# A transformer trunk on one core: four weight sums of the down projection move from VectorE to POOL, and the last three k tiles of the last product are taken result by result

## The chip, the cores and the metric

The kernel runs on one core of one Trainium2 chip. The metric is the device time of one execution in microseconds. The engines named below are TensorE (PE, matrix products), VectorE (DVE), ScalarE (ACT), GpSimd (POOL) and SyncE (SP, which issues the DMAs here).

## The reference

One layer of a hybrid decoder trunk on x of 2048 tokens by 1024 features, in f32: a mixer (matrix memory, attention and spatial gating side by side), and then a feed-forward network with a causal convolution, both gated and added to x. What matters here is the end of it:

```python
D_FF = 11 * D_MODEL // 4                      # 2816
def conv_ffn(h, w_up, w_conv, b_conv, w_down):
    z = h @ w_up
    z = causal_depthwise_conv(z, w_conv, b_conv)
    a, gv = jnp.split(z, 2, axis=-1)
    return (jax.nn.silu(a) * gv) @ w_down
...
        h = rms_norm(x, g_ffn[l]) * (1.0 + sc2) + sh2
        x = x + gt2 * conv_ffn(h, w_up[l], w_conv[l], b_conv[l], w_down[l])
```

The down projection is the last matrix product, (2048 x 2816) by (2816 x 1024).

## The kernel before

The tokens are taken in two halves H of 1024. For each half, class `Down` computes the product of the activations (1024 x 2816) and the weight (2816 x 1024) as a 2 x 2 block product with seven block products in place of eight (Strassen's scheme in Winograd's form). A block of activations is named (i, j): i is the block of 512 tokens, j the half of the 2816 rows of the sum. A quarter of the weight is (i, j) with i the half of those rows and j the block of 512 output columns. The products run in the order 1, 2, 7, 6, 5, 4, 3, and each runs over KH = 11 k tiles of 128 rows. One step is one (H, product p, k tile).

To keep f32 accuracy, each operand tile (128 x 512) is split into a high half (rounded, by ACT, `A.copy`, L1489) and a low half (the rest, by DVE, L1490), and `mm3` (L54 to L56) makes three matmuls: high by high, high by low, low by high. A step has four results i (128 tokens each, one PSUM bank each) of three matmuls: 12 matmuls a step, 132 a product.

Four methods share a step's work:

- `load` issues the DMAs of the weight tiles, tag `wd`, eight buffers; product 7 needs two tiles to a step, the others one.
- `prep` makes the two operands and their halves. Products 1 and 2 take them as they were loaded. Product 7 takes the difference of two activation blocks (L1468, into `sw`) and of two weight quarters (L1470, into `t2w`, one tile for each k tile, kept). Product 6 changes activations in place (L1473, L1474) and adds a weight quarter to `t2w` (L1475). Products 5 and 4 subtract `t2w` from the loaded weight tile in place (L1478, L1481). Product 3 changes activations in place (L1484). All these run on DVE. The halves lie in tag `wsp`, twelve buffers, four to a step.
- `mm` makes the matmuls. Product 3 goes on summing in the banks of product 5.
- `post` queues what is done with a finished product's results: product 1's are copied by ACT (L1543); those of 2, 5 and 4 take three DVE instructions each (L1524 with one operand from PSUM, L1528, L1529) and a store; those of 7 one (L1549, from PSUM); those of 6 four (L1554 and L1555, from PSUM, L1579, L1580); those of 3 two (L1568, from PSUM, L1569) and a store to `out`.

The main loop (L1659 on) walks the steps: loads six steps ahead, `prep` three steps ahead (AHEAD = 3), then the matmuls, then up to three queued pieces of the results. A scheduler orders each engine's instructions by this order and by its own estimates of time, and allots the buffers of each tag. After the last step the four results of product 3 are finished (`last`, L1565 to L1570).

Of the kernel before, what the change touches and what calls it, by code (L numbers as in the profile page):

```python
# [12 lines left out]
ALU = mybir.AluOpType  # L13
# [20 lines left out]
def trunk(  # L34
# [7 lines left out]
    V, A, G, T = nc.vector, nc.scalar, nc.gpsimd, nc.tensor  # L42
# [10 lines left out]
    def mm3(ps, lh, ll, rh, rl, start, stop, resume=False):  # L53
        T.matmul(ps, lh, rh, start=start, stop=False, skip_group_check=resume)  # L54
        T.matmul(ps, lh, rl, start=False, stop=False, skip_group_check=resume)  # L55
        T.matmul(ps, ll, rh, start=False, stop=stop, skip_group_check=resume)  # L56
# [266 lines left out]
    def half2(tag):  # L323
        return (
            pool.tile([P, 512], F32R, name=tag + "h", tag=tag),
            pool.tile([P, 512], F32R, name=tag + "l", tag=tag),
        )
# [273 lines left out]
    def products(i, mm):  # L601

        w = nxt[0]
        for k in range(KT):
            mm(k)
            if k == 3 and wide[0]:
                tick(True)
            if w and i == 7:
                if k in (0, 1, 2, 5):
                    w.cast()  # L610
                if k == 0:
                    w.load()
        if w and i <= 3:
            w.load()
        if w and 4 <= i <= 6:
            w.cast()
            w.load()
        tick()
# [16 lines left out]
    def natural(half, wb, consume):  # L635
        wide[0] = wb.width == 512
        for i in range(8):
            tt = half * 8 + i
            tb, o = tt // 4, (tt % 4) * P
            ps = acc_ps()  # L640

            def mm(k):
                hh, hl = hT[tb, k]
                mm3(ps[:, : wb.width], hh[:, o : o + P], hl[:, o : o + P], *wb.tiles[k], k == 0, k == KT - 1)

            products(i, mm)
            consume(tt, ps)
# [544 lines left out]
    class Block:  # L1192
# [10 lines left out]
        def mm(self, i, nb):  # L1203
            if i not in self.x:
                self.x[i] = pool.tile([P, D], F32, name="x2")
                dma(self.x[i], x[self.rows(i), :])
                self.st[i] = pool.tile([P, 2], F32, name="st", tag="wst_")
            sl = slice(i * P, (i + 1) * P)
            ps = self.ps[i, nb] = pp.tile([P, 512], F32, name="wps")
            for k in range(KT):  # L1210
                mm3(ps, self.y[k][0][:, sl], self.y[k][1][:, sl], *wo[nb * 8 + k], k == 0, k == KT - 1)
# [116 lines left out]
    class Group:  # L1328
# [12 lines left out]
        def prep(self, p):  # L1341
            A_ = self.A
            n = OF[p]
            if (self.H, self.g) == (0, 0) and (0, n) not in hb:
                b_first(n)
            if p in (5, 6) and self.S1 is None:
                self.S1, self.S2 = self.tmp("S1", "sw"), self.tmp("S2", "sw")
                V.tensor_tensor(self.S1, A_[2, 1], A_[2, 2], op=ALU.add)
                V.tensor_tensor(self.S2, self.S1, A_[1, 1], op=ALU.subtract)
            if p == 7:  # L1350
                V.tensor_tensor(self.S1, A_[1, 1], A_[2, 1], op=ALU.subtract)
            elif p == 3:
                V.tensor_tensor(self.S2, A_[1, 2], self.S2, op=ALU.subtract)
            src = {1: A_[1, 1], 2: A_[1, 2], 4: A_[2, 2]}.get(p)
            if src is None:
                src = self.S1 if p in (5, 7) else self.S2
            hi, lo = half2("wsp")
            A.copy(hi, src)  # L1358
            V.tensor_tensor(lo, src, hi.bitcast(F32), op=ALU.subtract)  # L1359
            self.wa[p] = hi, lo  # L1360
# [67 lines left out]
    KH = 11  # L1428
    n_bank = [0]

    class Down:
# [29 lines left out]
        def prep(self, p, k):  # L1461
            a = lambda i, j: self.act(i, j, k)
            B = self.B.pop((p, k))
            if p in (1, 2):
                av, bv = a(1, p), B[0]
            elif p == 7:
                av = self.tmp("sw")
                V.tensor_tensor(av, a(1, 1), a(2, 1), op=ALU.subtract)  # L1468
                bv = self.T2[k] = self.tmp("t2w")
                V.tensor_tensor(bv, B[0], B[1], op=ALU.subtract)  # L1470
            elif p == 6:

                V.tensor_tensor(a(2, 1), a(2, 1), a(2, 2), op=ALU.add)  # L1473
                V.tensor_tensor(a(1, 1), a(2, 1), a(1, 1), op=ALU.subtract)  # L1474
                V.tensor_tensor(self.T2[k], self.T2[k], B[0], op=ALU.add)  # L1475
                av, bv = a(1, 1), self.T2[k]
            elif p == 5:
                V.tensor_tensor(B[0], B[0], self.T2[k], op=ALU.subtract)  # L1478
                av, bv = a(2, 1), B[0]
            elif p == 4:  # L1480
                V.tensor_tensor(B[0], B[0], self.T2[k], op=ALU.subtract)  # L1481
                av, bv = a(2, 2), B[0]
            else:
                V.tensor_tensor(a(1, 2), a(1, 2), a(1, 1), op=ALU.subtract)  # L1484
                av, bv = a(1, 2), B[0]
            halves = []
            for v in (av, bv):
                hi, lo = half2("wsp")
                A.copy(hi, v)  # L1489
                V.tensor_tensor(lo, v, hi.bitcast(F32), op=ALU.subtract)  # L1490
                halves += [hi, lo]
            self.sl[p, k] = halves

        def mm(self, p, k):
            more = p == 3
            if k == 0:
                if more:
                    self.ps[3] = self.ps[5]
                else:
                    n_bank[0] += 1  # L1500
                    tag = "db%d" % ((n_bank[0] - 1) % 2)
                    self.ps[p] = [pp.tile([P, 512], F32, name="db", tag=tag) for _ in range(4)]
            ah, al, bh, bl = self.sl.pop((p, k))
            for i in range(4):
                sl = slice(i * P, (i + 1) * P)
                mm3(self.ps[p][i], ah[:, sl], al[:, sl], bh, bl, not more and k == 0, k == KH - 1, resume=more)

        def rest(self, ti, nl, i):

# [134 lines left out]
    for i in range(AHEAD):  # L1644
        up_groups(-1)
    prep(0)
    blk.evict(2, 1)
    blk.stats(2)
    prep(1)
    blk.scale(2, True)  # L1650
    blk.evict(3, 1)
# [3 lines left out]
    blk.scale(3, True)  # L1655
    b_first("B21", (3,))
    prep(2)
    loaded = n_open + 1
    for i, s in enumerate(steps):  # L1659
# [86 lines left out]
```

## Time and profile before

| | |
|---|---|
| median of 3 runs | 2607.7 us (2606.87 to 2610.26) |
| profiled execution, time | 2607.8 us |
| profiled execution, span | 2606.1 us |
| granted TensorE clock, mean | 0.997 |
| PE busy | 2530.5 us (97%) |
| DVE busy | 2010.0 us (77%) |
| ACT busy | 1272.8 us (49%) |
| POOL busy | 402.5 us (15%) |

The span runs from the first instruction to the end of the last; the time of the profiled execution is 1.7 us longer and is the one to set beside the median. Busy times overlap between engines. Matmuls are pipelined and their ends are modelled, so that each shows 0.39 us although the next one begins 0.23 us after it. A line L54 to L56 is that of the helper `mm3`, so groups are told apart by their tiles: `db` is the down projection's result, `wsph` and `wspl` its high and low halves, `act` its activations, `wd` and `t2w` its weight tiles.

### The profile page before, as it was taken

The page shows a single profiled execution, that of the slowest core. Times are in us where ns is not written, and L with a number is a line of the kernel's source. Part 1 is how long each engine was busy: PE and PEld are TensorE (multiplying, and loading weights), DVE is VectorE, ACT ScalarE, POOL GpSimd, SP SyncE. Part 2 cuts the span into 40 slices and gives each one's busy share as a digit, 9 for nine tenths or more (in the row PEclk, how much of TensorE's full clock was granted, in tenths as well). Part 3 has the DMA queues.
Part 4 walks back from the last instruction along what each step waited for, and adds up shares of the span by engine and source line. Part 5 has one row for each costly group of instructions (what it writes and reads, how often), then busy time and mean ns, then how long its engine had stood idle before and what let it go on. Part 6 is the DMA issues. An engine that isn't in the chain of part 4 may idle for free.

```text
span 2606.1 us, 36311 instructions
## 1 busy us (share of the span) xinstructions
PE 2530.5 (97%) x12521; PEld 2097.9 (81%) x12537; DVE 2010.0 (77%) x3438; ACT 1272.8 (49%) x2424; POOL 402.5 (15%) x532
## 2 busy tenths in 40 slices
PE   5999999999999999999989999999999999999999
PEld 5888888888787877777868888888888888888787
DVE  7657666476388889866589888888888887997797
ACT  4333343432388878844455544454444444444443
POOL 2012310132266556520000000000000000000000
PEclk9999999999999999999999999999999999999999
DMA  7345763454664445266632222255222217658523
GB/s 247 107 120 160 209 209 88 129 152 138 180 164 123 129 126 166 58 195 224 248 89 92 79 89 82 81 201 187 90 81 81 90 65 279 210 176 290 184 93 117
DMA packets 302592, 379.58 MB, mean 146 GB/s; under 512 B 31934, under 2 KB 194588, under 8 KB 300360
## 3 DMA queue, kind: packets, MB, share of 16 engines
q1 hardware_dynamic: 302408, 377.26, 46.1%
q8 instruction: 99, 1.62, 0.3%
q14 instruction: 85, 0.70, 0.1%
HBM read 276.44 MB, written 100.74 MB: 145 GB/s over the span
## 4 chain that ended last, share of the span: by engine, by line
PE 81%; DVE 9%; DMA 4%; ACT 3%; issue 2%; POOL 1%; SPq 0%; DVEq 0%; ACTq 0%; POOLq 0%
PE ub L56 11%; PE ub L54 11%; PE ub L55 11%; PE acc L54 6%; PE acc L56 6%; PE acc L55 6%; PE db L55 4%; PE db L56 4%; PE db L54 4%; PE sp L206 3%; PE tp L259 3%; PE op L245 2%; PE op L246 2%; PE wps L55 2%; PE wps L54 2%
## 5 line engine op out<-in xcount | busy, mean ns | idle before, releaser
L54 PE MATMUL acc<-wh,hh 128*128 128x512 f32 (+2 forms) x768 | 285.5, 373 | 1.9 <-DVE vhl L762 1.2
L54 PE MATMUL ub<-T,wsph 128*128 128x512 f32 x704 | 274.2, 390 | 5.8 <-ACT wsph L1358 5.8
L56 PE MATMUL ub<-T,wspl 128*128 128x512 f32 x704 | 273.7, 389 | 1.6 <-DVE wspl L1359 1.6
L56 PE MATMUL acc<-wh,hl 128*128 128x512 f32 (+2 forms) x768 | 274.2, 360 | 0.3 <-DVE hl L566 0.3
L55 PE MATMUL acc<-wl,hh 128*128 128x512 f32 (+2 forms) x768 | 273.9, 358 | 0.2
L55 PE MATMUL ub<-T,wsph 128*128 128x512 f32 x704 | 273.9, 389 | 0.0
L55 PE MATMUL db<-wspl,wsph 128*128 128x512 f32 x616 | 240.6, 391 | 3.6 <-DVE wspl L1490 3.5
L56 PE MATMUL db<-wsph,wspl 128*128 128x512 f32 x616 | 239.6, 389 | 0.0
L54 PE MATMUL db<-wsph 128*128 128x512 f32 x616 | 238.3, 389 | 0.3 <-ACT wsph L1489 0.3
L1358 ACT CAST wsph<-S 128x512 fp32r<-128x512 f32 x176 | 109.7, 623 | 228.4 <-PE ub L55 162.8
L263 DVE TENSOR_TENSOR plo<-tp,phi 128x512 fp32r<-128x512 f32 (+1 forms) x320 | 187.0, 607 | 31.6 <-ACT phi L262 29.4
L54 PE MATMUL ub<-B,wsph 128*128 128x512 f32 x528 | 207.1, 392 | 2.8 <-ACT wsph L1358 2.8
L56 PE MATMUL ub<-B,wspl 128*128 128x512 f32 x528 | 207.2, 392 | 0.6 <-DVE wspl L1359 0.6
L55 PE MATMUL ub<-B,wsph 128*128 128x512 f32 x528 | 207.0, 392 | 0.0
L223 ACT ACTIVATE L<-L,nm 128x1024 f32<-128x1024 f32 (+2 forms) x192 | 172.6, 903 | 36.0 <-DVE nm L212 34.7
L262 ACT CAST phi<-tp 128x512 fp32r<-128x512 f32 (+1 forms) x320 | 160.0, 521 | 40.2 <-PE tp L259 38.9
L259 PE MATMUL tp<-ident,L 128*128 128x128 f32 x1088 | 177.0, 274 | 2.5 <-POOL L L228 0.6
L206 PE MATMUL sp<-kk,q 128*128 128x512 f32 (+3 forms) x640 | 169.2, 375 | 3.3 <-DVE nm L212 2.2
L1489 ACT CAST wsph<-act 128x512 fp32r<-128x512 f32 x132 | 82.3, 623 | 179.0 <-PE db L55 162.2
L228 POOL TENSOR_SCALAR L<-L,rs 128x1024 f32<-128x1024 f32 (+2 forms) x192 | 167.2, 881 | 11.0
L56 PEld LDWEIGHTS acc<-wh,hl 128*128 128x128 f32 x768 | 145.0, 190 | 22.3 <-DVE hl L566 0.8
L54 PEld LDWEIGHTS acc<-wh,hh 128*128 128x128 f32 x768 | 146.2, 191 | 20.7 <-DVE vhl L762 1.4
(333 smaller groups left out, 5942.9 us busy)
## 6 DMA issues: line engine op xcount, KB each, us to landing
w<-in_w_up_dram SPq DMA_DIRECT2D x88, 512.0 KB
wd<-in_w_down_dram SPq DMA_DIRECT2D x176, 256.0 KB
wa<-in_w_ada_dram SPq DMA_DIRECT2D x96, 256.0 KB
act_d<-yc SPq DMA_DIRECT2D x44, 512.0 KB
act<-act_d SPq DMA_DIRECT2D x44, 512.0 KB
wr<-in_w_in_dram SPq DMA_DIRECT2D x64, 256.0 KB
q<-q_d SPq DMA_DIRECT2D x128, 128.0 KB
hc_d<-hl SPq DMA_DIRECT2D x28, 512.0 KB
```

Source lines behind the costliest of these rows:

```text
L54: T.matmul(ps, lh, rh, start=start, stop=False, skip_group_check=resume)
L55: T.matmul(ps, lh, rl, start=False, stop=False, skip_group_check=resume)
L56: T.matmul(ps, ll, rh, start=False, stop=stop, skip_group_check=resume)
L206: T.matmul(sp[:, b : b + bw], q2[n][:, qs], kk[:, s0 + b : s0 + b + bw], start=n == 0, stop=n == 1 and not last)
L223: A.activation(L[c], L[c], AF.Exp, bias=nm[:, n - 1 : n], scale=-1.0, accum_out=rs[:, c : c + 1])
L228: G.tensor_scalar(t, t, rs[:, 0:1], 1.0, op0=ALU.mult, op1=ALU.mult)
L245: T.matmul(op[:, c0:], vv[:, j, :], hi[:, c0:], start=(j == 0), stop=False)
L259: T.transpose(tp[:, i * P : (i + 1) * P], rows[i][j // 8][:, (j % 8) * P : (j % 8 + 1) * P], ident)
L262: A.copy(hi[:, c0:], tp[:, c0:])
L263: V.tensor_tensor(lo[:, c0:], tp[:, c0:], hi[:, c0:].bitcast(F32), op=ALU.subtract)
L1358: A.copy(hi, src)
L1489: A.copy(hi, v)
```

## The change

The four kinds of weight sums of products 7, 6, 5 and 4 are issued to POOL in place of DVE, with the same operands. In product 3 of the second half of the tokens, the steps of k tiles 8 and 9 issue no matmuls; the step of k tile 10 issues those of all three tiles, ordered by result: for each of the four results, tiles 8, 9 and 10 with three matmuls each.

```diff
                 bv = self.T2[k] = self.tmp("t2w")
-                V.tensor_tensor(bv, B[0], B[1], op=ALU.subtract)
+                G.tensor_tensor(bv, B[0], B[1], op=ALU.subtract)
             elif p == 6:
 
                 V.tensor_tensor(a(2, 1), a(2, 1), a(2, 2), op=ALU.add)
                 V.tensor_tensor(a(1, 1), a(2, 1), a(1, 1), op=ALU.subtract)
-                V.tensor_tensor(self.T2[k], self.T2[k], B[0], op=ALU.add)
+                G.tensor_tensor(self.T2[k], self.T2[k], B[0], op=ALU.add)
                 av, bv = a(1, 1), self.T2[k]
             elif p == 5:
-                V.tensor_tensor(B[0], B[0], self.T2[k], op=ALU.subtract)
+                G.tensor_tensor(B[0], B[0], self.T2[k], op=ALU.subtract)
                 av, bv = a(2, 1), B[0]
             elif p == 4:
-                V.tensor_tensor(B[0], B[0], self.T2[k], op=ALU.subtract)
+                G.tensor_tensor(B[0], B[0], self.T2[k], op=ALU.subtract)
                 av, bv = a(2, 2), B[0]
...
-            ah, al, bh, bl = self.sl.pop((p, k))
+            ks = [k]
+            if more and self.H == 1 and k > KH - 4:
+                ks = range(KH - 3, KH) if k == KH - 1 else ()
+            got = [self.sl.pop((p, j)) for j in ks]
             for i in range(4):
                 sl = slice(i * P, (i + 1) * P)
-                mm3(self.ps[p][i], ah[:, sl], al[:, sl], bh, bl, not more and k == 0, k == KH - 1, resume=more)
+                for j, (ah, al, bh, bl) in zip(ks, got):
+                    mm3(self.ps[p][i], ah[:, sl], al[:, sl], bh, bl, not more and j == 0, j == KH - 1, resume=more)
```

## The prediction

> **What bounds the kernel now.** The page first: TensorE (PE) is busy for 97% of the span and holds 81% of the chain that ended last. A change can gain only where PE waits, and it loses wherever it makes PE wait.
>
> ```profile
> PE 2530.5 (97%) x12521; PEld 2097.9 (81%) x12537; DVE 2010.0 (77%) x3438; ACT 1272.8 (49%) x2424; POOL 402.5 (15%) x532
> PE 81%; DVE 9%; DMA 4%; ACT 3%; issue 2%; POOL 1%; SPq 0%; DVEq 0%; ACTq 0%; POOLq 0%
> ```
>
> The change touches the down projection alone, the last stage. So next comes the view by windows of 30 us there (columns: PE, weight load, VectorE (DVE), ScalarE, POOL, granted clock, DMA share, GB/s).
>
> ```profile
> 2210.00:2240.00 30.00, 30.00 (x134) 24.83 (x133) 22.44 (x38) 12.65 (x24) 0.00 (x0) 1.00 0.80 286
> 2240.00:2270.00 30.00, 30.00 (x134) 24.86 (x133) 30.00 (x51) 13.20 (x24) 0.00 (x0) 1.00 0.66 211
> 2270.00:2300.00 30.00, 30.00 (x134) 24.82 (x133) 30.00 (x51) 13.17 (x23) 0.00 (x0) 1.00 0.41 133
> 2300.00:2330.00 30.00, 29.22 (x128) 23.55 (x127) 30.00 (x51) 12.14 (x21) 0.00 (x0) 1.00 0.46 148
> ...
> 2420.00:2450.00 30.00, 28.30 (x121) 22.13 (x121) 18.27 (x30) 11.42 (x20) 0.00 (x0) 1.00 0.68 220
> 2450.00:2480.00 30.00, 28.61 (x124) 22.67 (x123) 30.00 (x51) 11.23 (x20) 0.00 (x0) 1.00 0.49 158
> 2480.00:2510.00 30.00, 30.00 (x134) 24.86 (x133) 30.00 (x51) 12.57 (x22) 0.00 (x0) 1.00 0.19 61
> 2510.00:2540.00 30.00, 30.00 (x134) 24.82 (x134) 30.00 (x51) 12.73 (x23) 0.00 (x0) 1.00 0.42 133
> ```
>
> Three things are to be seen. PE at full pace does 134 matmuls in 30 us. DVE is full for 90 us in each half of the tokens, at 51 instructions in 30 us, 0.60 us from start to start; these are products 7, 6 and 5. PE nearly keeps its pace all the same: three windows fall short, by 6, 13 and 10 matmuls. At 0.227 us each (the last fence below has 35 spacings from 2591.65 to 2599.58 us) that is 29 x 0.227 = 6.6 us, and with the tail this is all that can be won here.
>
> The waits of this stage say who made PE wait:
>
> ```profile
> PE db L55 <- DVE wspl L1490: 3.5, 5, 1.2
> DVE t2w L1470 <- DMA wd<-in_w_down_dram: 9.6, 8, 2.5
> ```
>
> PE waits for DVE's low halves (L1490). The view counts only 3.5 us, since it lets each matmul end late; the missing matmuls give 6.6. In 2420 to 2450 DVE isn't full: it stands in L1470 before a weight tile that hasn't landed, with low halves that PE needs queued behind it.
>
> **The sums move to POOL.** Four groups leave DVE, 22 instructions each, 88 in all, 44 in each half:
>
> ```profile
> L1481 DVE TENSOR_TENSOR wd<-wd,t2w 128x512 f32<-128x512 f32 x22 | 15.2, 697 | 0.0
> L1475 DVE TENSOR_TENSOR t2w<-t2w,wd 128x512 f32<-128x512 f32 x22 | 15.2, 691 | 0.0
> L1470 DVE TENSOR_TENSOR t2w<-wd 128x512 f32<-128x512 f32 x22 | 15.2, 690 | 9.6 <-DMA wd<-in_w_down_dram 9.6
> L1478 DVE TENSOR_TENSOR wd<-wd,t2w 128x512 f32<-128x512 f32 x22 | 15.2, 693 | 0.0
> ```
>
> At 0.60 us each, DVE is freed of 26.4 us in each half. POOL is idle here (0.00 in every window above). What POOL asks for the same shape, and what it does to DVE meanwhile, is seen earlier in the span, where both engines split the output weights (three stretches, each engine's own timeline: start, duration):
>
> ```profile
> 1138.99 1.30 POOL L132 TENSOR_TENSOR wo1l<-ld,wo1h 128x512 fp32r<-128x512 f32 x1 [10.04 <-ACT wo1h L131]
> 1139.00 0.69 DVE L1217 TENSOR_TENSOR yg<-wps,gt 128x512 f32<-128x512 f32 x1 [3.62 <-ACT wo1h L131]
> 1139.72 1.11 DVE L1218 TENSOR_TENSOR x<-x,yg 128x512 f32<-128x512 f32 x1
> ...
> 1144.95 1.29 POOL L132 TENSOR_TENSOR wo1l<-ld,wo1h 128x512 fp32r<-128x512 f32 x1 [4.66 <-ACT wo1h L131]
> 1145.15 1.64 DVE L1218 TENSOR_TENSOR x<-x,yg 128x512 f32<-128x512 f32 x1
> ...
> 1125.96 2.99 POOL L132 TENSOR_TENSOR wo1l<-ld,wo1h 128x512 fp32r<-128x512 f32 x2 [8.48 <-ACT wo1h L131]
> 1126.43 1.38 DVE L132 TENSOR_TENSOR wo1l<-ld,wo1h 128x512 fp32r<-128x512 f32 x1 [2.29 <-ACT wo1h L131]
> ```
>
> POOL takes 1.30 us. DVE's L1217, one of whose operands (wps) lies in PSUM, takes its 0.69 us beside it. L1218, both of whose operands lie in SBUF, doesn't: twice it ends 0.54 to 0.55 us after POOL's end (1140.83 after 1140.29, 1146.79 after 1146.24), whenever it had begun. So it stood until POOL was through. The third stretch shows the other direction: DVE ends at 1127.81 and POOL's second at 1128.95, 1.14 us later, although its first was through at 1127.26. Two-operand instructions out of SBUF on the two engines exclude each other.
>
> The Trainium skill has this rule twice, in two widths. "Advanced Engine Details and Errata", section "Mode Summary", names only VectorE instructions in a mode with two read ports, and "VectorE: DVE Perf Modes", section "Why tensor_tensor can't do 2×_2P or 4×", says that this instruction can't be in one; by these the sums would cost DVE nothing and the second rival's 2600.0 us would come out. "GPSIMD Engine Reference", section "Key points", adds VectorE instructions with two SBUF inputs, and by it the forecast stands. The three stretches bear out the wider rule: L1218 is a tensor_tensor, and it stood.
>
> Does POOL come in between two DVE instructions of a full queue? DVE is full here, so this matters.
>
> ```profile
> 269.79 1.90 DVE L596 TENSOR_TENSOR wl<-wr,wh 128x512 fp32r<-128x512 f32 x3
> 269.96 2.01 POOL L128 TENSOR_TENSOR ss<-ss,nhalf 128x8 f32<-128x8 f32 x1 [6.33 <-DVE ss L771]
> ...
> 276.91 0.69 DVE L596 TENSOR_TENSOR wl<-wr,wh 128x512 fp32r<-128x512 f32 x1
> 277.08 2.02 POOL L128 TENSOR_TENSOR ss<-ss,nhalf 128x8 f32<-128x8 f32 x1 [4.53 <-DVE ss L771]
> ```
>
> Behind three DVE instructions back to back POOL needs 2.01 us, behind one 2.02. It waits for the instruction that runs and goes in front of the next. So in a full DVE queue one POOL sum makes the way from one DVE end to the next 1.14 + 0.55 = 1.69 us in place of 0.60: it costs DVE x = 1.1 us, where the instruction taken off DVE had cost 0.60. The bounds of x: above, POOL's whole 1.30. Below: some sums fall beside DVE instructions that read PSUM (L1524, L1549, L1554, L1555), of which the code has 4, 4, 8 and 4 in products 7, 6, 5 and 4. If all 20 were used, 20 x 0.60 = 12 us over 44 sums come off, 0.27 each, and x is 0.83. I take 1.1: DVE's order isn't written to line these up.
>
> The sum, product by product. PE needs 132 x 0.227 = 29.9 us for each. DVE has left (from the code, by 0.60): product 7, 11 differences, 22 low halves and 12 instructions for product 2's results, 45, 27.0 us; product 6, 22 + 22 + 4 = 48, 28.8; product 5, 22 + 16 = 38, 22.8; product 4, 22 + 12 = 34, 20.4; product 3, 45, 27.0. With 11 sums in each of the first four, 11 x 1.1 = 12.1 us, they come to 39.1, 40.9, 34.9 and 32.5. Over PE's time that is 9.2 + 11.0 + 5.0 + 2.6 = 27.8 us in each half. Two things absorb part of it. The halves are prepared three steps ahead (12 wsp buffers, four to a step), 3 x 2.72 = 8.2 us. And eight wd buffers let four of product 7's sums run during product 2, where DVE has room (22.44 and 18.27 us of 30): 4 x 1.1 = 4.4. What is left, 15.2 us, PE waits, 30.4 in both halves. The old 6.6 us are replaced: DVE no longer stands before a landing tile, and the DVE backlog is in the new sum.
>
> New waits: ScalarE's casts of t2w and wd (L1489) wait for POOL where they waited for DVE, with the next casts queued behind them and through these DVE's low halves and PE. A sum of 1.3 us in place of 0.69 is 0.6 us later, inside the lead of three steps; once the lead is gone it is in x. On SP, loads into wd wait for POOL to read; POOL's only queue is these sums, so they are free sooner or as soon. I price this at nothing; without cover it would be 0.6 us for a step that waits.
>
> **The last three k tiles, result by result.** Nothing is added, 36 matmuls change order.
>
> ```profile
> 2591.62 0.62 ACT L1489 CAST wsph<-act 128x512 fp32r<-128x512 f32 x1 [1.58 <-PE db L55]
> 2591.65 0.39 PE L54 MATMUL db<-wsph 128*128 128x512 f32 x1
> 2592.89 0.69 DVE L1490 TENSOR_TENSOR wspl<-wd,wsph 128x512 fp32r<-128x512 f32 x1
> 2597.97 1.37 DVE L1568 TENSOR_TENSOR o<-db,gt 128x512 f32<-128x512 f32 x2 [4.39 <-PE db L56]
> 2599.26 1.28 DVE L1569 TENSOR_TENSOR o<-o,s 128x512 f32<-128x512 f32 x2
> 2599.58 0.39 PE L56 MATMUL db<-wsph,wspl 128*128 128x512 f32 x1
> 2600.46 1.28 DVE L1568 TENSOR_TENSOR o<-db,gt 128x512 f32<-128x512 f32 x2
> 2601.66 1.28 DVE L1569 TENSOR_TENSOR o<-o,s 128x512 f32<-128x512 f32 x2
> ```
>
> Now the four results end within 2 us, and DVE needs eight instructions for them: it ends at 2602.94, 2.97 us after the last matmul (2599.97). After, results end 9 x 0.227 = 2.0 us apart, more than two instructions need, so only the last one's two stand behind PE: 2 x 0.69 = 1.4. Gain 1.6. Against it: tile 10's buffers come free only when tile 7 ends (the cast at 2591.62), its last low half is there at 2593.58, and the first result now wants it seven matmuls after 2591.65, at 2593.24. PE waits 0.35. Net gain 1.2 us, if DVE has no backlog there: in product 3 it needs 27.0 of 29.9 us and its last eight steps hold three instructions (1.8 of 2.72 us), so the lead comes back.
>
> **Sum.** +30.4 - 6.6 - 1.2 = +22.6 us. The profiled execution took 2607.8 us (span 2606.1), 0.1 from the median of 2607.7. Forecast 2630.4 us.
>
> **The rivals.**
> 1. The bounds of x. At 1.3 the four products exceed PE by 11.4 + 13.2 + 7.2 + 4.8 = 36.6; less 8.2 and 5.2 that is 23.2, 46.4 for both, and with the gains +38.6: 2646.4 us. At 0.83 the products are over by 6.2, 8.0, 2.0 and -0.4, together 15.8; less 8.2 and 3.3 that is 4.3, or 8.6 for both, and with the gains +0.8: 2608.6. The repeated 0.55 us behind POOL's end speaks for 1.1; that low halves wait for ScalarE now and then, which leaves gaps, speaks for less.
> 2. POOL's sums fall into DVE's gaps and cost it nothing, so that the 26.4 us are a true relief: PE never waits, -6.6 - 1.2, 2600.0 us. It wins below the x at which a half loses no more than its share of the gains, 3.9 us: products 7, 6 and 5 give 78.6 + 33x - 89.7 - 8.2 - 4x = 3.9, x = 0.80. For it: DVE's idle time and the wait in L1470 at 2420 to 2450. Against: 90 us of full DVE in each half, and the three stretches above.
> 3. The order at the end hurts: DVE is still behind in product 3, tile 10 comes last, and behind it stand 29 matmuls (6.6 us) where 12 stood (2.7): 3.9 us lost in place of 1.2 won, 2635.5 us. The lead speaks against it.
>
> **How the numbers follow.** The mechanism with x near 1.1 gets 0.63, the low half of x (0.83 to 0.95) 0.18, the late tile 10 0.11, the true relief 0.08. The likeliest gives 2630.4. The range runs from x = 0.83, 2609, to x = 1.3 with the late tile, 2646.4 + 5.1, 2651. A measurement of this kernel can tell about 0.2%, 5.2 us, from no change. Faster by more is the relief alone, 0.08; within it lies about a third of the low half of x, 0.06; slower 0.86.
>
> **What would show it.** Right: POOL busy some 114 us or more (88 x 1.30), with means above 1.30 us; DVE's L1490 and L1468 means well above 0.69; PE short of matmuls in products 7, 6 and 5 of both halves, some 67 in each, with L1490 as the one waited for; L1470's wait for landing tiles on POOL, not on DVE. At the end two DVE instructions after the last matmul. Wrong: L1490's mean still at 0.69 with POOL at work beside it, or PE at 134 in every window.

## Result: slower by 1.8%, and the profile after

| | before | changed |
|---|---|---|
| median of 6 runs each | 2606.2 us | 2651.9 us (2650.9 to 2657.5) |
| ratio, 95% interval | 1 | 1.0177 (1.0163 to 1.0190) |
| profiled execution, span | 2606.1 us | 2649.5 us |
| from the down projection's first matmul to the end of its last | 428.5 us | 472.5 us |
| from there to the end of the span | 6.1 us | 4.5 us |

The forecast was 2630.4, range 2609 to 2651: the direction was right, the loss twice the size, just outside the range. All of the loss lies in the down projection (+44.0 us); the tail gains 1.6. One execution each of two experiments below lay far off (7006.7 us with all activation sums held back, 3154.6 us with product 4's sums alone); the ratios leave them out.

The changed kernel's page, engines and chain. POOL is at work for 177 us more, PE's share of the chain falls from 81 to 77%, and DVE's and POOL's rise:

```profile
PE 2546.8 (96%) x12537; PEld 2104.0 (79%) x12537; DVE 2031.4 (77%) x3350; ACT 1271.8 (48%) x2424; POOL 579.6 (22%) x620
PE 77%; DVE 11%; DMA 4%; issue 3%; ACT 3%; POOL 2%; SPq 0%; ACTq 0%; DVEq 0%; POOLq 0%
```

The windows of 30 us (columns as before: PE, weight load, DVE, ACT, POOL, granted clock, DMA):

```profile
2240.00:2270.00 30.00, 25.51 (x106) 19.11 (x105) 28.16 (x40) 9.56 (x17) 24.80 (x7) 1.00 0.46 150
2270.00:2300.00 30.00, 21.26 (x69) 15.48 (x68) 30.00 (x24) 6.35 (x11) 28.85 (x18) 0.83 0.42 132
2300.00:2330.00 30.00, 29.42 (x128) 23.67 (x127) 24.82 (x37) 12.56 (x22) 5.50 (x4) 1.00 0.40 129
2330.00:2360.00 30.00, 27.91 (x116) 22.57 (x115) 28.66 (x36) 10.46 (x19) 21.08 (x11) 0.94 0.68 222
...
2480.00:2510.00 30.00, 22.71 (x85) 16.95 (x84) 30.00 (x37) 7.76 (x14) 21.07 (x10) 0.89 0.48 157
2510.00:2540.00 30.00, 24.94 (x102) 19.67 (x101) 30.00 (x35) 10.04 (x18) 23.32 (x11) 0.94 0.13 44
```

Where PE did 134 matmuls it now does 69 to 106 in the four worst windows, and DVE does 24 to 37 instructions in a full window where it did 51. Two things there were not in the forecast: the loss is bunched (the next window, 2300 to 2330, is nearly back at pace with DVE not full), and the granted clock falls to 0.83 where PE waits most.

The waits and the groups of the sums. PE waits for L1490 as forecast, and the wait for landing tiles has gone to POOL (898.1 of its 1013.8 us are POOL's idle time before the stage). By their means the sums take 1.6 to 2.3 us each in place of 1.30, and L1490 on t2w 1.00 in place of 0.69:

```profile
POOL t2w L1470 <- DMA wd<-in_w_down_dram: 1013.8, 16, 898.1
...
PE db L55 <- DVE wspl L1490: 32.1, 20, 3.8
```

```profile
L1475 POOL TENSOR_TENSOR t2w<-t2w,wd 128x512 f32<-128x512 f32 x22 | 49.6, 2273 | 7.3 <-DVE wspl L1490 7.3
L1470 POOL TENSOR_TENSOR t2w<-wd 128x512 f32<-128x512 f32 x22 | 49.3, 2246 | 1014.1 <-DMA wd<-in_w_down_dram 1013.8
L1490 DVE TENSOR_TENSOR wspl<-t2w,wsph 128x512 fp32r<-128x512 f32 x44 | 44.1, 1003 | 1.8 <-ACT wsph L1489 1.8
...
L1478 POOL TENSOR_TENSOR wd<-wd,t2w 128x512 f32<-128x512 f32 x22 | 35.5, 1624 | 47.8 <-DMA wd<-in_w_down_dram 26.0 <-DVE wspl L1490 21.8
```

DVE's and POOL's own timelines in product 7 and 6 (start, duration) show both things that can happen when the two engines meet:

```profile
2250.26 16.94 POOL L1470 TENSOR_TENSOR t2w<-wd 128x512 f32<-128x512 f32 x1 [4.63 <-DMA wd<-in_w_down_dram]
2267.15 14.80 POOL L1475 TENSOR_TENSOR t2w<-t2w,wd 128x512 f32<-128x512 f32 x9
...
2267.88 1.11 DVE L1490 TENSOR_TENSOR wspl<-t2w,wsph 128x512 fp32r<-128x512 f32 x1 [1.84 <-ACT wsph L1489]
2268.92 1.77 DVE L1474 TENSOR_TENSOR act<-act 128x512 f32<-128x512 f32 x1
2270.62 1.78 DVE L1490 TENSOR_TENSOR wspl<-act,wsph 128x512 fp32r<-128x512 f32 x1
...
2267.23 0.62 ACT L1489 CAST wsph<-t2w 128x512 fp32r<-128x512 f32 x1 [4.19 <-POOL t2w L1470]
```

From 2268.92 on the engines take turns, and DVE needs 1.70 us from start to start: the forecast's 1.69. But the sum before, asked for at 2250.26, stood for 16.94 us while DVE ran on without a break. Only when ACT had waited 4.19 us for that sum, and DVE had run dry behind ACT (1.84 us), did POOL come in.

One window over the whole down projection gives the account that the rest hangs on. First for a kernel with the new tail alone (the first experiment below), then for the changed one:

```profile
2174.93:2600.29 425.36, 423.21 (x1861) 348.31 (x1859) 378.06 (x615) 182.32 (x315) 0.00 (x0) 1.00 0.58 199
```

```profile
2172.48:2644.94 472.46, 440.31 (x1861) 353.84 (x1859) 398.93 (x527) 181.03 (x315) 176.25 (x88) 0.97 0.53 179
```

The sums make it 47.1 us longer. DVE is busy for 20.9 us more (378.06 to 398.93), although 88 x 0.60 = 52.8 us of work has left it: so POOL held it up for 73.7 us, 0.84 for each sum. And DVE is idle for 26.2 us more (47.3 to 73.5). The forecast had only the first kind of loss.

PE's loss and DVE's idle time don't lie in the same places. From the first matmul of each product to that of the next, products 7 and 6 hold 41.2 of the 47.1 us (36.6 and 46.1 us in the first half, 42.8 and 37.3 in the second; with the tail alone 29.9, 29.9, 31.9 and 29.9). DVE is idle there for 12.2 us, of which 1.84 are the wait behind ACT above and the rest lies at the end of product 6, behind PE's last wait. Another 12.6 us lie in product 4 (2.4 with the tail alone), where PE keeps its pace (31.2 and 30.0 us). During PE's 20 waits for L1490 (32.1 us) DVE is never idle. What it stands for when it is idle is seen in the waits, and in the timelines of ACT and DVE at the end of product 6: it waits for ACT, and ACT waits until PE has read the halves whose buffers it needs. Then the lead of three steps is full. For POOL's results ACT waits only twice, for 4.8 us in all.

```profile
ACT wsph L1489 <- PE db L55: 239.5, 134, 7.2
...
ACT wsph L1489 <- POOL t2w L1470: 4.2, 1, 4.2
...
ACT wsph L1489 <- POOL t2w L1475: 0.6, 1, 0.6
```

```profile
2309.59 0.62 ACT L1489 CAST wsph<-act 128x512 fp32r<-128x512 f32 x1 [1.58 <-PE db L55]
...
2310.24 0.69 DVE L1490 TENSOR_TENSOR wspl<-act,wsph 128x512 fp32r<-128x512 f32 x1 [1.42 <-ACT wsph L1489]
```

### The profile page after: what moved, and what is told of

The parts are those of the page before. It is cut to its first block, busy times and chain, and to the rows that moved or that the text cites. A ratio compares the mean times of both kernels' runs of the same rounds, so it can differ in the third digit from the quotient of the medians.

```text
span 2649.5 us, 36446 instructions
## 1 busy us (share of the span) xinstructions
PE 2546.8 (96%) x12537; PEld 2104.0 (79%) x12537; DVE 2031.4 (77%) x3350; ACT 1271.8 (48%) x2424; POOL 579.6 (22%) x620
## 4 chain that ended last, share of the span: by engine, by line
PE 77%; DVE 11%; DMA 4%; issue 3%; ACT 3%; POOL 2%; SPq 0%; ACTq 0%; DVEq 0%; POOLq 0%
PE ub L56 10%; PE ub L54 10%; PE ub L55 10%; PE acc L54 6%; PE acc L56 6%; PE acc L55 6%; PE db L55 4%; PE db L56 3%; PE db L54 3%; PE sp L206 3%; PE tp L259 3%; DVE wspl L1490 3%; PE op L245 2%; PE op L246 2%; PE wps L54 1%
## 5 line engine op out<-in xcount | busy, mean ns | idle before, releaser
L55 PE MATMUL db<-wspl,wsph 128*128 128x512 f32 x616 | 247.3, 402 | 32.1 <-DVE wspl L1490 32.1
L1470 POOL TENSOR_TENSOR t2w<-wd 128x512 f32<-128x512 f32 x22 | 49.3, 2246 | 1014.1 <-DMA wd<-in_w_down_dram 1013.8
L55 PEld LDWEIGHTS db<-wspl,wsph 128*128 128x128 f32 x616 | 117.9, 191 | 67.7 <-DVE wspl L1490 43.6
```

## The experiments

Two theories. **A**: each sum costs DVE its price, and beside it only the order of DVE's queue matters (the scheduler puts work that isn't urgent ahead of low halves that are). **B**: POOL, shut out of DVE's unbroken row, delivers late, and the late result stops ACT, DVE and PE. Each ratio is to the kernel before as it ran beside that experiment (medians 2606.2 to 2608.7 us). Lengths and busy times come from one profiled execution of each kernel.

**The two edits alone.** The new tail without the moved sums (L1470, L1475, L1478, L1481 back on `V`):

> Only the order of the last three k tiles is changed; the four sums stay on VectorE. Both theories: the last matmul keeps its time to within 0.4 us and only the last result's two VectorE instructions stand behind it, so 1.2 to 1.6 us under before, a ratio of about 0.9995. Should the first result wait for tile 10, the last product takes up to 3.9 us longer instead.

Measured: 2604.1 us, 0.9994 (0.9985 to 1.0003). The trace has the tail at 4.5 us in place of 6.1; in time that isn't told from no change. Sums alone, with the old tail:

> Only the sums are on POOL; the last tiles are taken as before. Both theories: all of the loss and none of the tail's gain, 1.5 us above the changed kernel, about 2653 us beside its 2652. If the new order at the end had a part in the loss, this comes out well below 2652.

Measured: 2653.5 us, 1.0179 (1.0165 to 1.0192). The sums are the loss.

**One operand on POOL.**

```diff
-                G.tensor_tensor(bv, B[0], B[1], op=ALU.subtract)
+                G.tensor_scalar(bv, B[0], ones[:, 0:1], 1.0, op0=ALU.mult, op1=ALU.mult)
```

and so for the three other sums.

> As the changed kernel, but each sum is a POOL instruction of the same shape with one tensor input: it only copies the loaded tile, and the second operand is left out. By the page such an instruction holds POOL 0.69 us instead of 1.30. Theory A (POOL and VectorE exclude each other, each sum costs VectorE its port time): x falls from 1.1 to about 0.5 us a sum, below the 0.80 at which the change breaks even, so 2598 to 2612 us, most of the loss gone. Theory B (what costs is that POOL is kept out for 14 to 17 us behind VectorE's unbroken queue and its late result then stops ScalarE): the waiting stays whatever the length of the sum, at least 2630 us.

Measured: 2612.3 us, 1.0021 (1.0012 to 1.0030). With a cheaper instruction at the same places 39.6 us of the 45.7 go, to the upper edge of theory A's range. But the long waits, which theory B took to stay, went with the price: no POOL instruction lasts more than 3.0 us in this kernel. So the run doesn't tell the two apart. A little remains, though DVE now has 28 us less to do than with the tail alone (349.7 us busy).

**Product 3's sums held back.** In the changed kernel DVE's queue had product 3's seven L1484 moved from product 4 into product 6, between the low halves for which PE stood:

```profile
2292.58 1.76 DVE L1484 TENSOR_TENSOR act<-act 128x512 f32<-128x512 f32 x1
2294.27 1.75 DVE L1490 TENSOR_TENSOR wspl<-t2w,wsph 128x512 fp32r<-128x512 f32 x1
2295.94 3.46 DVE L1484 TENSOR_TENSOR act<-act 128x512 f32<-128x512 f32 x2
...
2296.07 0.50 PE L55 MATMUL db<-wspl,wsph 128*128 128x512 f32 x1 [2.12 <-DVE wspl L1490]
```

```diff
-                V.tensor_tensor(a(1, 2), a(1, 2), a(1, 1), op=ALU.subtract)
+                with tc.issue_after(self.low[(3, k - 5) if k > 4 else (4, k + 6)]):
+                    V.tensor_tensor(a(1, 2), a(1, 2), a(1, 1), op=ALU.subtract)
```

`self.low` keeps each step's last L1490.

> As the changed kernel, but product 3's activation sums (L1484) are issued no earlier than behind the low half of five steps before, which takes them out of product 6, where VectorE has no time. Theory A with the order of VectorE's queue as the missing part: PE's waits in product 6 fall by 4 to 6 us in each half, together 8 to 10 us, to about 2642 us. Theory B: VectorE's order has no part in it, 2650 to 2654 us.

Measured: 2640.5 us, 1.0138 (1.0109 to 1.0167). So the order is a cost of its own, as theory A had it; one of the four executions took 2653.5 us, though, and the interval just touches that of the changed kernel. In its window of the down projection DVE is as busy as in the changed kernel, and 8.7 us less idle (463.95 - 399.16 = 64.8):

```profile
2171.59:2635.54 463.95, 436.59 (x1861) 351.01 (x1859) 399.16 (x527) 180.76 (x315) 182.21 (x88) 0.99 0.52 182
```

**Fewer sums.** Product 7's alone on POOL (22 of 88):

> The new tail, and of the four quarter sums only product 7's (the 11 at L1470 in each half) on POOL; the 33 others of each half are DVE's as before. Product 7 is the first to use a quarter, and DVE has some lead over PE when it begins. Theory A (each POOL sum takes a price of about 1.1 us of DVE's time in place of 0.60, and what makes it dear is that DVE's queue is filled up with later sums as well): 22 x 0.5 us = 11 us more for DVE in all, of which the lead (8.2 us a half in the forecast) takes most, and product 7's own wait of 1 to 4 us in the kernel before stays; 2600 to 2608 us. Theory B (POOL is shut out by DVE's unbroken stream and its late results stop ACT and PE): the same stretches of 14 to 17 us stand in product 7, and the time is 2610 us or more.

Measured: 2613.3 us, 1.0024 (1.0013 to 1.0035), within theory B's 2610 or more: the down projection is 8.7 us longer than with the tail alone (DVE 5.1 busy, 3.7 idle), and one sum, of 22, stood for 17.0 us. Product 4's alone:

> The new tail, and of the four quarter sums only product 4's (L1481, 22 in all) on POOL. By the forecast's account by products, DVE needs 27.0 us of product 4's 29.9 with its sums, and 32.5 with POOL's at 1.1 us each, 2.6 more than PE, inside the lead of 8.2: no cost, 2602 to 2607 us. If each sum costs its net price of 0.46 us wherever it stands: 2604 + 10 = 2614. If moving sums makes the scheduler fill DVE's queue with other work at the cost of urgent halves: above 2607 too, with PE's waits in products 7 and 6 rather than 4.

Measured: 2624.2 us, 1.0058 (1.0041 to 1.0075): a down projection 19.9 us longer than with the tail alone, for 22 sums in a product where the forecast's account had room. It misses the account (2602 to 2607) and the bare price (2614), and the third expectation, waits in products 7 and 6: PE lost its time in product 4, 39.1 and 39.7 us for 29.9. Here is what happened, in the timelines of POOL and ACT, and then the window of the down projection:

```profile
2304.75 36.89 POOL L1481 TENSOR_TENSOR wd<-wd,t2w 128x512 f32<-128x512 f32 x11 [981.91 <-DVE s L1583]
...
2325.19 0.62 ACT L1489 CAST wsph<-wd 128x512 fp32r<-128x512 f32 x1 [4.55 <-POOL wd L1481]
```

```profile
2171.59:2616.87 445.28, 431.49 (x1861) 351.60 (x1859) 381.20 (x593) 182.44 (x315) 72.38 (x22) 0.98 0.56 190
```

The first of the eleven sums stood from 2304.75 for 20.4 us. ACT's cast, and all casts behind it, waited for it; DVE meanwhile did seven L1484 that nobody needed yet, and then ten sums came in one burst. Over the down projection DVE is hardly busier than with the tail alone (+3.1 us) but 16.8 us more idle, nearly none of it while PE waits. So the bare price isn't enough here; the first sum's lateness and the order both show in the trace, and the next run takes the order away.

**Product 4's sums with product 3's held back** (both edits above):

> Product 4's sums alone on POOL, as in the run that gave 2624.2 us, and product 3's activation sums (L1484) issued no earlier than behind the low half of five steps before. In the run without the hold these seven in each half stood in product 5, one product earlier than with all sums on DVE. Theory A with order as a cost: 2 x 7 x 0.61 = 8.5 us come off, and what is left is the bare price of 22 sums, 22 x 0.46 = 10 us over the 2604.1 of the new tail alone: 2612 to 2618 us. If the order isn't a cost of its own and being shut out is: 2620 to 2626 us.

Measured: 2616.4 us, 1.0031 (1.0022 to 1.0041), as theory A had it. The down projection is 6.4 us shorter by the order alone (438.9; DVE 8.8 less idle, 2.4 more busy), although sums still stood for 7.7 and 13.5 us. The intervals with and without the hold just touch here too, but both pairs of kernels point the same way.

**All activation sums held back.**

```diff
+                with self.behind(p, k, 2):
                     V.tensor_tensor(av, a(1, 1), a(2, 1), op=ALU.subtract)
...
+                with self.behind(p, k, 2 if k > 3 else k + 20):
                     V.tensor_tensor(a(2, 1), a(2, 1), a(2, 2), op=ALU.add)
                     V.tensor_tensor(a(1, 1), a(2, 1), a(1, 1), op=ALU.subtract)
```

`behind` names the last L1490 so many steps before.

> The changed kernel with all activation sums of the down projection held near their steps: for k tiles 4 to 10 those of products 6 (L1473, L1474) behind the low halves of two steps before, those of product 3 (L1484) behind the low half of five steps before; L1468 of all tiles behind two steps before. Theory A, with order as a cost of its own: only the price is left, 88 sums x (1.07 - 0.61) = 40 us less what products 5, 4 and 3 can absorb; about 2626 to 2636, 5 us or more under the 2640.5 of the run in which product 3's sums alone were held. Theory A with product 3's sums as the only harmful ones: 2638 to 2643. Theory B (POOL's late results are what costs): no change from the changed kernel's order would help, 2645 or more.

Measured: 2659.8 us, 1.0190 (1.0170 to 1.0209), not told from the changed kernel, with a down projection 7.3 us longer in the trace (479.8). Both readings of theory A miss, by 17 us or more; theory B's 2645 or more holds. Work done early had a use too: DVE's idle time in product 1 rose from 4.8 to 10.6 us in the first half and from 9.1 to 11.8 in the second, and what it had done there now stood in product 7. Early work was bad here in a full product and good in an idle one. The same holds on the one-operand kernel:

> The kernel with one-operand instructions on POOL in place of the sums (the second operand of each weight sum is left out), which gave 2612.3 us, and now the same holds on DVE's activation sums as in the kernel above. A one-operand instruction of POOL held DVE's row up by 0.42 us, less than the 0.61 us that DVE is freed of, so DVE has less to do than with the new tail alone (2604.1). Order as a cost of its own: the 8 us between the two go, 2598 to 2606. If the 8 us are not order: 2609 to 2614.

Measured: 2611.6 us, 1.0011 (1.0002 to 1.0021), no gain over 2612.3: those 8 us are not this order. Product 7 loses some 5 us in each half there, and in the first half POOL had run 18 of its 44 instructions in it, ahead of need; whether that is the cause wasn't tried.

**When does POOL come in?** Three small kernels apart, one execution each: rows of DVE instructions out of SBUF with one instruction on POOL:

> Nothing of the model is computed here: the output is a copy of x, and in front of the end stand eight short sections on 128x512 float32 tiles. In each DVE has a row of 16 independent instructions and POOL a sum (in the last but one four sums, in the last a one-operand instruction) that becomes ready with the first of them. Theory B (POOL's large instruction waits until DVE's row is broken): with two-operand sums from SBUF, POOL's sum ends only behind the row, about 16 x 0.6 = 9.6 us after it is ready; with a tiny store behind each fourth, or each fourth reading PSUM, it starts at the first of these, after about 2.4 us; in the row of one-operand copies it starts at once; each instruction of DVE behind which POOL gets in starts about 1.2 us later. What the forecast had written (POOL waits for the DVE instruction that runs and goes in front of the next): POOL's sum ends about 1.9 us after it is ready in every section with two operands, whatever the length of the row. Theory A says nothing on when POOL gets in, only that DVE's row is 1.1 us longer with each POOL sum in it.

Measured: POOL came in at once in all sections (its end 1.77 us after its operand, 1.26 in the row of copies), DVE's row of 16 took 10.79 us with one sum in it and 9.72 beside POOL's store, which holds nothing up (1.07 for a sum). Four small stores made such a row 0.04 us longer. Theory B's rule fell, as put there. But every one of these sums came at a row's first instruction. So they were made to come later:

> Nothing of the model is computed: the output is a copy of x, with seven sections on 128x512 float32 tiles in front of the end. DVE has a row of 24 instructions in each, and POOL's instruction needs the output of the fourth (in the second section the tenth), so that it comes in the middle of the row, not at its first instruction as in the sections before. Theory B's rule (in the middle of an unbroken row of two-operand instructions POOL stands until the row breaks): POOL ends behind the row, 20 x 0.6 = 12 us after its operand, 14 x 0.6 = 8.4 in the second; at the break (DVE's fourteenth: a one-operand copy, one with an operand in PSUM, or a tiny store behind it) 10 x 0.6 = 6 us. The rule of the forecast (it waits for the one that runs): 1.8 us in each. In the row of one-operand copies 1.3 us by both.

Measured: 1.64 us behind number 3, in all four sections with a sum there, and 9.47 behind number 9. The border:

> Nothing of the model is computed: the output is a copy of x, with nine short sections in front of the end. DVE has a row of 24 instructions of two operands in each, and POOL's instruction needs the output of number 4, 5, 6, 7 or 8 of the row (counted from 0). In four more sections it needs number 9's, and number 13 is a one-operand copy, or one with an operand in PSUM, or has a small store behind it, or POOL's is a one-operand instruction. Before, POOL came in at once behind number 3 (1.64 us) and stood 9.47 us behind number 9, until the row's end. If what decides is how long the row has run: from one of the numbers 4 to 8 on POOL stands until the row ends, 18 to 15 x 0.6 = 11 to 9 us. If it is chance: long and short ones mix. With a break at number 13 POOL should end about 4 x 0.6 + 1.3 = 3.7 us after its operand where the break opens the way, and 9.5 us where it doesn't.

Measured (the two kernels' timelines: POOL behind number 3 in the first; behind number 4, then behind number 9 with a PSUM operand and with the small store at number 13, in the second):

```profile
9.20 13.19 DVE L58 TENSOR_TENSOR om<-bm,xs 128x512 f32<-128x512 f32 x20
9.37 1.64 POOL L58 TENSOR_TENSOR pm<-fm,xs 128x512 f32<-128x512 f32 x1 [8.92 <-DVE fm L58]
```

```profile
9.82 11.53 DVE L58 TENSOR_TENSOR om<-bm,xs 128x512 f32<-128x512 f32 x19
9.99 12.47 POOL L58 TENSOR_TENSOR pm<-fm,xs 128x512 f32<-128x512 f32 x1 [9.55 <-DVE fm L58]
...
111.25 2.85 POOL L58 TENSOR_TENSOR ppsum<-fpsum,xs 128x512 f32<-128x512 f32 x1 [13.32 <-DVE fpsum L58]
...
127.09 3.45 POOL L58 TENSOR_TENSOR ptiny<-ftiny,xs 128x512 f32<-128x512 f32 x1 [12.99 <-DVE ftiny L58]
```

Behind the fourth instruction of a row POOL comes in at once; behind the fifth it stands until the row is over (12.47 us; 11.88, 11.27, 10.67 and 10.07 behind the sixth to ninth: always to the row's end). A one-operand copy, an operand in PSUM or a small store at number 13 lets it in (2.84, 2.85 and 3.45 us, theory B's 3.7 or a little less). A one-operand instruction of POOL stands too (8.89 us). Each place from the fifth on was measured once or twice, and all agree: how long the row has run decides, not chance. (Whether what counts is its instructions or its time, a border between 2.6 and 3.2 us from its start, isn't told apart.)

The changed kernel shows the same in its second long sum. It was asked for at 2502.04 and stood while DVE ran on out of SBUF; it ended at 2516.37, 1.24 us after the start of the first DVE instruction there that reads PSUM (L1553):

```profile
2502.04 14.33 POOL L1475 TENSOR_TENSOR t2w<-t2w,wd 128x512 f32<-128x512 f32 x1 [3.64 <-DVE wspl L1490]
...
2515.13 0.68 DVE L1553 TENSOR_TENSOR u<-db,s 128x512 f32<-128x512 f32 x1
2515.73 1.19 DVE L1490 TENSOR_TENSOR wspl<-t2w,wsph 128x512 fp32r<-128x512 f32 x1
```

**DVE's row broken on purpose.** A store of zeros to a 128x1 tile behind each low half:

```diff
+                with tc.issue_after(getattr(ins, "ins", ins)):
+                    V.memset(junk, 0.0)
```

> The changed kernel with one more DVE instruction behind each low half (308 in all): a store of zeros to a tile of 128x1, which reads nothing from SBUF, so that DVE's stream of two-operand instructions is broken every second one. Theory B (POOL is shut out while that stream is unbroken, and what it delivers late is what costs the time): POOL's sums of 14 to 17 us go, and the time falls by 5 us or more below the changed kernel, to 2647 or less. Theory A (DVE has no time left; POOL's sums take it away whenever they come): 308 x 0.06 to 0.1 us = 18 to 31 us more of DVE's time, of which the stretches where DVE is late (about half of product 7 to 4 in each half) show; 2652 to 2675 us, even if the long POOL sums are gone.

Measured: 2661.4 us, 1.0207 (1.0191 to 1.0222). The time is in theory A's range. No sum takes more than 1.84 us any more, and still the down projection takes the 472 us that it took:

```profile
2186.20:2658.08 471.88, 439.26 (x1861) 353.59 (x1859) 410.26 (x832) 180.88 (x315) 138.63 (x88) 0.97 0.53 179
```

DVE is 11.9 us less idle than in the changed kernel (61.6 for 73.5) and 11.3 us more busy. Letting POOL in takes idle time away and pays for it in DVE's busy time. (The other 10 us of the median come before the down projection, which starts at 2186.2 us and not at 2172.5; see the end.) The same on product 4's sums alone, and with product 3's held back:

> Product 4's sums alone on POOL, as in the run that gave 2624.2 us, and behind each low half of the down projection one store of zeros to a tile of 128x1 (0.06 us; in the row of the small kernel it fitted between two instructions without moving the next one). In the run without it POOL's first sum of product 4 stood 20.4 us in one half and 18.9 in the other, ScalarE's cast and all behind it stood before that sum, and then ten sums came in one burst. Theory B (being shut out costs, by taking the lead away): POOL's long sums go, and with them most of the 18 us that product 4 lost: 2603 to 2611 us. Theory A (each sum has its price, wherever it stands, and the order of DVE's queue does the rest): no change, 2620 to 2626 us.

> The changed kernel with both: product 3's activation sums (L1484) issued no earlier than behind the low half of five steps before (k tiles 3 to 10; 0 to 2 are free), and the small store behind each low half. The hold alone gave 2640.5, the small stores alone left the down projection as long as in the changed kernel (471.9 us after 472.5) and moved its losses from product 6 to product 7. If the price of 88 sums at 1.07 in place of 0.61 us is what is left once queue order and shut-outs are gone, less what the forecast's account by products absorbs: about 2626 to 2634 us. If the shut-outs cost nothing here because DVE is full without a break anyway: 2637 to 2643 us, as with the hold alone.

Measured: 2631.7 us, 1.0089 (1.0072 to 1.0106), and 2660.7 us, 1.0201 (1.0185 to 1.0216). Both start the down projection 10 and 14 us late as well; by its length alone, product 4's is 442.7 us (445.3 without the stores; DVE 11.5 less idle, 8.8 more busy), the other 470.8 (464.0 with the hold alone). All expected numbers miss. In all three DVE's idle time falls by 4 to 12 us once POOL is let in, but taken away in this manner it is worth little or nothing: the stores cost DVE time too.

**The price with nobody waiting.** All sums on DVE, and 88 more on POOL whose results nothing reads:

```diff
+            if p in (7, 6, 5, 4):
+                G.tensor_tensor(self.tmp("spare"), B[0], B[0], op=ALU.add)
```

> The new tail, with all weight sums on DVE as before, and beside them 88 sums more on POOL (one in each step of products 7, 6, 5 and 4; each adds a step's weight tile to itself, into a tile that nothing reads). No cast and no matmul waits for POOL; only the buffer of a weight tile stays taken until POOL has read it. Theory A (a two-operand sum on POOL takes 1.07 us of DVE's time, whoever needs its result): some 12 to 14 fall into DVE's idle time in product 2, 74 x 1.07 = 79 us for the others, all of it seen by PE since DVE is full through these four products: 2604 + 79 = 2683 us, 2665 to 2695. Theory B (POOL's late results are the cost, and a POOL that is shut out takes nothing from DVE): 2604 to 2615 us.

Measured: 2652.8 us, 1.0164 (1.0149 to 1.0179); both theories miss.

```profile
2171.86:2646.36 474.50, 439.00 (x1861) 351.62 (x1859) 422.21 (x615) 182.87 (x315) 183.86 (x88) 0.98 0.52 178
```

The down projection is 49.1 us longer than with the tail alone, 44.2 of it DVE's busy time (422.21 - 378.06): 0.50 us for a sum, less than 1.07. In part this sum was cheaper from the start: with one tile as both operands POOL needs 1.04 us undisturbed, where it needed 1.30, and DVE 1.45 us from start to start in turns, so that a meeting costs 0.85. In part a POOL that is shut out and that nobody waits for slipped in where DVE reads PSUM (0.25 us more for the DVE instruction behind, at 2268.17 us) or stands anyway. In the changed kernel a sum cost 0.84, with the idle time on top; how much of this difference comes from somebody waiting isn't shown.

## Why the forecast was right in direction and wrong in size

- **Right: the exclusion and its price per meeting.** 1.70 us from start to start in turns (forecast 1.69), 1.07 us for a sum in the small kernel (x = 1.1). L1490 on t2w shows it as asked for, 1003 ns, and POOL's groups a mean above 1.30. The relief rival (2600.0) is out, and so is the late tile 10: the tail gained what it should.
- **Mis-sized: how many meetings.** Forecast 80 x 1.1 = 88 us of DVE's time (four early sums in each half taken off). Measured 73.7, 0.84 for each of 88: where DVE reads PSUM, a sum cost it 0.50 (a pair of L1553 and L1490 takes 1.70 us from start to start, in place of 1.20). With 73.7 in place of 88 the forecast's own account gives 30.4 - 14.3 = 16.1 us of waits and 2616.1; so it isn't this term that made the loss too small.
- **Wrong: "it waits for the instruction that runs and goes in front of the next".** It was read from two rows, of one and of three DVE instructions, and in both POOL's instruction came in the row's first 0.2 us. It is one of 128x8 that takes 1.64 us undisturbed (the median of 32), so it waited for 0.4. Short rows are just where the reading holds: up to the fourth instruction. In the down projection's full rows POOL stood for 14 to 17 us. The two rows could not have shown it; the error was to carry them to rows of fifty.
- **Wrong: the new wait of the casts "priced at nothing".** It was to be 0.6 us inside a lead of three steps, 8.2 us. Standing for 17 us takes that lead twice over, and ACT waited 4.19 us for one such sum and DVE 1.84 us behind it. But what this cost in all isn't shown: ACT's waits for POOL come to 4.8 us in the stage, and with the row opened, where no sum is late, the stage is as long.
- **Wrong: DVE full from product 7 to product 4, with the lead paid out once (15.2 us of waits in each half).** This is the step that made the loss too small. DVE stood idle for 28.4 us in these four products of both halves, 2.6 with the tail alone, and the loss came early: in products 7 and 6 DVE was busy for 150.6 us, with the tail alone for 121.6, where PE needs 119.7. PE waited there beyond the lead; the room that DVE had in product 4 came too late to be of use. So the waits came to 47.1 us over the tail alone, where the account with 73.7 us gives 16.1.
- **Wrong, and a part of it: the code's order taken as DVE's.** The account by products put product 3's sums in product 3. The scheduler, presumably since by its own estimates DVE was relieved, put seven of them in product 6, at up to 1.76 us each, and DVE stood idle in product 4 later. Holding them gave 11.4 us of the median back; 8.7 of the 26.2 us of idle time. It also put nine of product 6's pairs (L1473, L1474) into product 7, two with the tail alone; these were held only together with others, without a gain.
- **Missing: PE doesn't come back at full pace.** After its longest waits PE makes its matmuls 0.43 us apart, not 0.227, with a granted clock of 0.56 in that stretch (its timeline, and windows of 3 us):

```profile
2275.79 0.50 PE L55 MATMUL db<-wspl,wsph 128*128 128x512 f32 x1 [3.72 <-DVE wspl L1490]
...
2277.17 0.63 PE L56 MATMUL db<-wsph,wspl 128*128 128x512 f32 x1
2277.59 0.63 PE L54 MATMUL db<-wsph 128*128 128x512 f32 x1
```

```profile
2273.00:2276.00 3.00, 0.21 (x1) 0.21 (x2) 3.00 (x3) 0.00 (x0) 3.00 (x3) 1.00 0.54 168
2276.00:2279.00 3.00, 3.00 (x9) 2.33 (x9) 3.00 (x2) 0.00 (x0) 3.00 (x3) 0.56 0.54 170
```

  Of the down projection's spacings, 52 lie between 0.38 and 0.46 us in the changed kernel, together 10.3 us over full pace; with the tail alone there is none. Not all of it is lost: while PE is slow, DVE gains on it. The Trainium skill has this in "TensorE: Matmul & The Clock Gate", Part 1: an idle window of about 3.4 us halves the array's clock, and about as long of work brings it back. The trace agrees for this wait (3.72 us, then from 2276.36 to 2279.73 us, 3.4 us, eight matmuls at about half pace) and for two more, of 3.83 and 3.67 us; but three of the six such stretches began behind a wait of only 2.1 us, like the one at 2296.07 above, and behind two others of 2.0 and 2.1 us there was none.
- **Right: the tail.** 1.6 us less behind the last matmul; two DVE instructions there, as said.
- **The lead's credit, 8.2 + 4.4 us in each half.** Early sums are no credit of the change: with the tail alone DVE runs five and nine of its own L1470 in product 2's idle time, and POOL now five and seven. And the lead, to be used once over four products, was used up by product 6 and filled again at its end, where DVE stood idle for 5 us or more in both halves and PE had waited already.

What stays open: of the 26.2 us of DVE's idle time, holding product 3's sums took 8.7 away, opening the row 11.9, and both together 12.7 (73.5 - 60.8). For the other 13.5, and for why the loss falls into products 7 and 6 even with the row open, the runs don't say how much is the turns themselves, early work in the wrong place, or PE's halved clock. No run lets POOL in without adding to DVE's work. None of the versions beats the kernel before; the tail alone is the best and can't be told from it.

## What to carry to other kernels

Where VectorE was full and fed the critical path, giving its two-operand sums to POOL didn't pay: a meeting in a row out of SBUF costs VectorE more (1.07 us here) than the sum it is freed of (0.60), beside an instruction that reads PSUM less (0.50), and a POOL result that others wait for can come late on top. Look for an engine's price in the state in which it will work (a row of fifty instructions, not of three), and look at who waits for the result. Room that an engine has in a later stage doesn't repay a wait in an earlier one. Where a scheduler orders the queue, ask what it will put into the room that it believes it has won.

## What the runs showed that was not expected

- A row of DVE instructions with two SBUF operands shuts POOL out from its fifth on, to its end, whatever the length (15 to 19 more instructions, 10.1 to 12.5 us, in the small kernels). The Trainium skill, "SBUF — State Buffer", section "Who interferes with whom", says that the order of issue decides who blocks. Up to the fourth instruction the trace agrees; from the fifth on it doesn't, since POOL's instruction shows as begun (9.99 us, above) before ten and more DVE instructions that went in front of it. By that rule the forecast's "goes in front of the next" would have stood.
- A 0.06 us store in such a row opens it for POOL (3.45 us after its operand, where the rest of the row would have been 9.5).
- In the three kernels with that store the down projection began 10 to 14 us later. In all three the matmuls of the stage before stood further apart (437 or 438 in 100 us, for 442 or 443 in the changed kernel and in those without the store that were looked at, at a granted clock of 1.00). A tile of 128x1 more in SBUF is the only edit that reaches there. The start differs by some us among the other kernels too (2168.5 to 2177.8 us); the cause wasn't tried.
